# Seven block products in place of eight for most of the down-projection of a decoder layer, and the residual kept with tokens on partitions

## The chip, the core and the metric

The kernel runs on one core of one Trainium2 chip, in one launch. Its time is the device time of that core in microseconds; where several runs are given, their median. Five engines work side by side, each through its own queue in program order: TensorE (PE, with PEld for its weight loads), VectorE (DVE), ScalarE (ACT), GpSimd (POOL) and SyncE (SP, which issues all DMAs here). They wait for each other by semaphores.

## What is computed

One decoder layer on 256 tokens, with 16 meta tokens ahead of them as further keys: a norm, an input projection, eight heads of differential attention and eight of stick-breaking attention, an output projection and an MLP with a squared ReLU. D_MODEL is 2048 and D_FF 8192, all in float32.

```python
u = _rmsnorm(h, g_mix[l])
proj = jnp.einsum('bld,de->ble', u, w_in[l])
...
mixed = jnp.concatenate([o_diff, o_sb], axis=-1)
h = h + jnp.einsum('ble,ed->bld', mixed, w_out[l])

m = _rmsnorm(h, g_mlp[l])
hid = jnp.square(jax.nn.relu(jnp.einsum('bld,df->blf', m, w_up[l])))
h = h + jnp.einsum('blf,fd->bld', hid, w_down[l])
```

## The kernel before

**Float32 products in parts.** Each operand is split into a leading part `hi` (type fp32r) and the rest `lo`. A product is the sum of hi·hi, hi·lo and lo·hi. For the weights ACT makes `hi` by a cast (L164) and DVE makes `lo` by a subtraction (L166), for every tile that arrives.

**The weight stream.** All weights pass once through one stream of units, numbered in the order of use (list `order`). A unit is a tile of 128 partitions x 4 x 256 elements (512 KB): one DMA on SP into one of five buffers `raw` (RAW), then the split into one of three pairs `whi`, `wlo` (PARTS), then products. `fetch` and `later` (L203, L845) issue the load of a unit when the raw buffer five units back has been split. `part` and `halves` (L213, L220) issue the split of a unit when PE is done with the unit three back.

**The stages.** 24 strips of four units are the input projection, with attention woven in; 8 strips the output projection ("out"); then four rounds of 8 strips "up" and 8 strips "down" (ROUNDS = 4). In the last three kinds the weights are the stationary operand, and the moving operand has the tokens in its columns: `products` (L806) issues, for each 128x128 block of weights, one product of 512 columns (`whi` with both parts of the activation, side by side) and one of 256 (`wlo` with the leading part), so 768 columns. The result has output features on partitions. The residual is kept in the same form, in `xT` (features on partitions, tokens in the free dimension).

**Leaving PSUM.** PSUM has four banks "acc" for the stream and four "att" for attention. A strip uses two of "acc". `residual` (L714) adds both halves of a bank to `xT` with two DVE operations; `out_evac` (L724) then also makes `m` (the scaled operand of up, in two parts) and sums squares for the norm; `mlp_norm` (L743) makes the norm's factor `R2` as a row for each token; `up_evac` (L765) adds the halves, applies ReLU and R2, squares, and splits into `hid`; `down_evac` (L779) adds to the residual and in the last round sends 128 KB out for every 128 features.

**What sets the order.** Every engine issues in the order of the program, and that order comes from the planner `Pace` (L39). It keeps an estimated time for PE, DVE and ACT (`T`, `V`, `A`). The products of the stream are written one after another; between them `pump` writes the next steps of side jobs that are due by the estimates, trying the lanes in the order "fetch", "weights", "once", "evac", "head". So a due split of weights is written ahead of a due evacuation.

```python
    def V(self, n, rate=0.96, after=0.0):
        self.dve = max(self.dve, self.pe, after) + n / rate + 65
        return self.dve + self.WAIT
```

In `out`, the first two strips take turns (`units`), so that the last heads of attention have more products ahead of the first use of their result in `mixed`.

## Time and profile before

| what | value |
|---|---|
| median of 3 runs | 1163.44 us (1162.42 to 1163.62) |
| span of the profiled execution | 1161.0 us, first to last instruction of the core |
| time around that span | not in the profile; the median of the runs is 2.4 us above it |
| bytes read from HBM | 204.39 MB |
| input projection with attention | from the start to 340 us |
| output projection and MLP | 340 to 1157 us |

The page gives for each engine its busy time, the span in 40 slices, the chain of work that ended last, and the costliest groups of instructions by line. A row of the timeline has the start and the duration in us, the engine, the line, the operation, what is written from what is read, and the shape; in brackets stands the idle time before it and what ended that. Matmuls overlap in their records (a 256-wide one lasts 0.28 us and the next starts earlier), so the cost of one in a row is the distance between two starts. A row of the table of windows has the stretch, its length, the busy time of PE, PEld, DVE, ACT and POOL with the number of instructions, the granted clock of PE, the DMA share and the GB/s.

### The profile page before, as it was taken

The numbers are of one execution on the slowest core, as the hardware profiler recorded it, in microseconds if no ns is written. First come the engines' busy times: TensorE is split into PE (matmuls) and PEld (weight loads), VectorE is DVE, ScalarE is ACT, GpSimd is POOL, SyncE is SP. The second block draws the span as 40 slices with busy tenths as digits, with TensorE's granted clock in tenths as the row PEclk, the third lists the DMA queues.
The fourth block names the chain that finished last, engine by engine and source line by source line (L and its number), as shares of the span: only waits on it lengthen the run. The fifth ranks groups of instructions, "written<-read, shape, count | busy, mean of one in ns | idle before, by whom it ended". The sixth has DMA issues, their size and how long they took to land.

```text
span 1161.0 us, 18961 instructions
## 1 busy us (share of the span) xinstructions
PE 1153.8 (99%) x7393; PEld 1040.0 (90%) x7393; DVE 784.5 (68%) x1287; ACT 660.0 (57%) x1131; POOL 1.1 (0%) x8
## 2 busy tenths in 40 slices
PE   8999999999999999999999999999999999999998
PEld 7999999999998888888888888888888888888887
DVE  6998987887877767656555665555566555656654
ACT  7769888779675545554334554334555333555332
POOL 0000000000000000000000000000000000000000
PEclk9999999999999999999999999999999999999999
DMA  8544444444545555555555555555555555555662
GB/s 324 190 144 140 146 146 146 164 158 136 178 136 173 186 192 185 182 189 189 184 184 188 190 182 185 189 189 182 186 192 184 182 188 191 183 183 190 198 219 82
DMA packets 58986, 207.73 MB, mean 179 GB/s; under 512 B 6672, under 2 KB 8848, under 8 KB 58896
## 3 DMA queue, kind: packets, MB, share of 16 engines
q1 hardware_dynamic: 58896, 206.52, 51.5%
q8 instruction: 58, 0.95, 0.3%
q14 instruction: 32, 0.26, 0.1%
HBM read 204.39 MB, written 2.10 MB: 178 GB/s over the span
## 4 chain that ended last, share of the span: by engine, by line
PE 99%; DMA 0%; SPq 0%; DVE 0%; ACT 0%; issue 0%
PE acc L821 47%; PE acc L820 24%; PE acc L815 8%; PE acc L817 8%; PE acc L816 8%; PE s_d L539 1%; PE po_s L579 1%; PE po_d L579 1%; PE z_s L539 0%; DMA raw<-in_win 0%; PE pq_dq L467 0%; PE pv_s L516 0%; PE pv_d L516 0%; SPq L199 0%; PE pn_s L275 0%; PE pn_d L274 0%
## 5 line engine op out<-in xcount | busy, mean ns | idle before, releaser
L166 DVE TENSOR_TENSOR wlo<-raw,whi 128x1024 fp32r<-128x1024 f32 (+1 forms) x390 | 470.2, 1207 | 328.4 <-ACT whi L164 323.7
L164 ACT CAST whi<-raw 128x1024 fp32r<-128x1024 f32 (+1 forms) x390 | 403.5, 1036 | 428.9 <-PE acc L821 399.4
L821 PE MATMUL acc<-hid,whi 128*128 128x512 f32 x1024 | 357.5, 399 | 0.0
L821 PE MATMUL acc<-m,whi 128*128 128x512 f32 x1024 | 357.3, 398 | 0.0
L820 PE MATMUL acc<-hid,wlo 128*128 128x256 f32 x1024 | 277.2, 281 | 0.0
L820 PE MATMUL acc<-m,wlo 128*128 128x256 f32 x1024 | 277.2, 281 | 0.0
L815 PE MATMUL acc<-u,whi 128*128 128x272 f32 (+1 forms) x768 | 223.7, 291 | 2.0 <-ACT whi L164 2.0
L821 PEld LDWEIGHTS acc<-hid,whi 128*128 128x128 f32 x1024 | 188.3, 188 | 41.6
L821 PEld LDWEIGHTS acc<-m,whi 128*128 128x128 f32 x1024 | 188.3, 188 | 41.4
L817 PE MATMUL acc<-u,wlo 128*128 128x272 f32 (+1 forms) x768 | 220.1, 287 | 0.4 <-DVE wlo L166 0.4
L816 PE MATMUL acc<-u,whi 128*128 128x272 f32 (+1 forms) x768 | 219.7, 286 | 0.0
L820 PEld LDWEIGHTS acc<-hid,wlo 128*128 128x128 f32 x1024 | 193.3, 189 | 6.4
L820 PEld LDWEIGHTS acc<-m,wlo 128*128 128x128 f32 x1024 | 193.3, 189 | 6.4
L815 PEld LDWEIGHTS acc<-u,whi 128*128 128x128 f32 x768 | 144.8, 189 | 3.6 <-ACT whi L164 2.7
L817 PEld LDWEIGHTS acc<-u,wlo 128*128 128x128 f32 x768 | 144.7, 188 | 1.0 <-DVE wlo L166 1.0
L816 PEld LDWEIGHTS acc<-u,whi 128*128 128x128 f32 x768 | 145.2, 189 | 0.0
L821 PE MATMUL acc<-mixed,whi 128*128 128x512 f32 x256 | 89.8, 399 | 0.0
L820 PE MATMUL acc<-mixed,wlo 128*128 128x256 f32 x256 | 69.3, 281 | 0.0
L821 PEld LDWEIGHTS acc<-mixed,whi 128*128 128x128 f32 x256 | 47.1, 188 | 10.1
L820 PEld LDWEIGHTS acc<-mixed,wlo 128*128 128x128 f32 x256 | 48.3, 189 | 1.5
L767 ACT COPY ut<-acc 128x256 f32<-128x256 f32 x64 | 23.7, 370 | 15.2 <-PE acc L821 15.2
L773 DVE SCALAR_TENSOR_TENSOR ut<-ut,R 128x256 f32<-128x256 f32 x64 | 27.0, 422 | 1.1
(400 smaller groups left out, 795.2 us busy)
## 6 DMA issues: line engine op xcount, KB each, us to landing
raw<-in_wup SPq DMA_DIRECT2D x128, 512.0 KB, 3.3
raw<-in_wdn SPq DMA_DIRECT2D x128, 512.0 KB, 3.3
raw<-in_win SPq DMA_DIRECT2D x95, 512.0 KB, 3.4
raw<-in_wout SPq DMA_DIRECT2D x32, 512.0 KB, 3.3
out<-xT SPq DMA_DIRECT2D x16, 128.0 KB, 1.7
xT<-in_x SPq DMA_DIRECT2D x3, 544.0 KB, 8.8
cst<-in_cst SPq DMA_DIRECT2D x1, 673.0 KB, 10.3
xT<-in_x SPq DMA_DIRECT2D x2, 272.0 KB, 3.5
```

Source lines behind the costliest of these rows:

```text
L164: nc.scalar.copy(hi, src)
L166: nc.vector.tensor_tensor(lo, src, as32(hi), op=ALU.subtract)
L539: nc.tensor.matmul(dst, lhsT=q[x][rows, cols], rhs=k[y][rows, :n], start=i == 0, stop=i == 2)
L579: nc.tensor.matmul(o, lhsT=l, rhs=r, start=i == 0, stop=i == len(todo) - 1)
L767: nc.scalar.copy(t, o[:, SEQ:])
L773: nc.vector.scalar_tensor_tensor(t, t, 0.0, R2, op0=ALU.max, op1=ALU.mult)
L815: nc.tensor.matmul(o, lhsT=h, rhs=xh, start=first, stop=False)
L816: nc.tensor.matmul(o, lhsT=h, rhs=xl, start=False, stop=False)
L817: nc.tensor.matmul(o, lhsT=l, rhs=xh, start=False, stop=last)
L820: one = lambda: nc.tensor.matmul(out[j][:, SEQ:], lhsT=l, rhs=act[:, k, 0, :], start=False, stop=False)
L821: two = lambda: nc.tensor.matmul(out[j], lhsT=h, rhs=act[:, k, :, :], start=first, stop=last)
```

## The change

**Down in eight rounds, with seven products for eight.** ROUNDS becomes 8 (each of 1024 hidden features), and a round is split into four column groups u of 512 output features. In the first three groups of rounds 0 to 6 (`FAST`) the 2x2 blocks (two token halves, two column halves, two halves of the contraction) are multiplied by Strassen's scheme: seven block products. The activations are now the stationary operand (128 tokens), the weights the moving one, and the result has tokens on partitions. A block product is three matmuls of 256 columns (`triple`). The fourth group and the whole of round 7 stay plain: three matmuls of 512 columns for each of four pairs.

The scheme needs sums of blocks. For the weights `fast_a` splits three blocks of a unit (768 elements), then makes four sums in place in `raw` by three DVE operations; `fast_b` splits those four sums as a second unit of the stream, without a load of its own. For the activations `up_evac` makes four sums by three DVE operations and splits eight blocks instead of four. The seven results of a group are kept in an SBUF tile Z[u] over the rounds: `fast_evac` copies (round 0, ACT) or adds (DVE) four banks "att" into it. After round 6 `combine` forms the four blocks from the seven (seven DVE operations) and adds them to the residual, scaled by R2 (four more).

**Tokens on partitions.** The residual is a new tile H (two halves of 128 tokens x 2048 features), loaded once more from HBM as a separate input of 2 MB. The out products have activations as stationary operand too, three matmuls of 512 columns. `out_evac` adds to H, sums squares on ACT, transposes H by PE (32 of 128x128) and makes `m` from the transposes. R2 is now one factor for each token, applied where down is added to H, not before the square: R2 is squared already there (no root is taken).

**Up** has weights stationary as before, now as three matmuls of 256 columns (`triple2`). Up of round r+1 and down of round r take turns in the stream, in each group: up, up, down, up, down, up, down, down.

**Buffers and planner.** From the MLP on there are four parts instead of three, and a lead of three units. The estimates of `V` and `A` carry 140 and 180 ns for each operation instead of 65 and 93, and a product 0.461 ns for a column. In the output projection the strips no longer take turns.

```diff
-ROUNDS = 4
+ROUNDS = 8
+PAIRS = 4
+MLP_PARTS = 4
+MLP_LEAD = 3
+FAST = {(r, u) for r in range(ROUNDS - 1) for u in range(3)}
...
+    for r in range(ROUNDS):
+        for u in range(4):
+            for c, p in (((0, 1), (0,)), ((2,), (1,)), ((3,), (2, 3))):
+                order += up(r + 1, u, c) + down(r, u, p)
...
+    def fast_a(g, hi, lo):
+        while (g, 0) not in raw_at or ring[g] >= 0 and ring[g] not in done_at:
+            yield pc.pe + 200, None
+        yield max(raw_at[g, 0], done_at.get(ring[g], 0.0)), "a"
+        raw = raws[g]
+        t = yield from split(hi[:, 1:4], lo[:, 1:4], raw[:, 1:4], 768)
...
+        first = raw[:, 0:1].to_broadcast([P, 2, 256])
+        nc.vector.tensor_tensor(raw[:, 3::-3], first, raw[:, 3:1:-1], op=ALU.add)
+        pc.V(512)
+        nc.vector.tensor_tensor(raw[:, 2], raw[:, 3], raw[:, 2], op=ALU.add)
+        pc.V(256)
+        nc.vector.tensor_tensor(raw[:, 1], raw[:, 2], raw[:, 1], op=ALU.add)
+        pc.at["sums", g] = pc.V(256)
+
+    def fast_b(g, hi, lo):
...
+        t = yield from split(hi, lo, raws[g - 1], 1024)
...
+    def up_evac(r, i, o):
+        x = mtile("hx", [P, FULL, P], f"hx_{r}_{i}", 2)
+        nc.scalar.activation(x[:, 0:4].rearrange("p a b -> p (a b)"), o, AF.Relu)
...
+        nc.scalar.activation(x[:, 0:4], x[:, 0:4], AF.Square)
...
+            nc.vector.tensor_tensor(x[:, 4:7:2], x[:, 0:2], x[:, 1:4:2], op=ALU.subtract)
+            nc.vector.tensor_tensor(x[:, 5], x[:, 4], x[:, 3], op=ALU.add)
+            nc.vector.tensor_tensor(x[:, 7], x[:, 2], x[:, 5], op=ALU.subtract)
...
+        nc.scalar.copy(hi, x)
+        nc.vector.tensor_tensor(lo, x, as32(hi), op=ALU.subtract)
...
+    def fast_evac(r, u, o):
+        for i in range(4):
+            n = 512 if i < 3 else 256
+            dst = z[:, 512 * i : 512 * i + n]
+            if new:
+                nc.scalar.copy(dst, o[i][:, :n])
+            else:
+                nc.vector.tensor_tensor(dst, o[i][:, :n], dst, op=ALU.add)
+            pc.give("att", t)
+        if r == LAST_FAST[u]:
+            yield from combine(u)
...
+    def triple(out, x, w, first, last, check=False):
+        for i, (a, b) in enumerate(((0, 0), (1, 0), (0, 1))):
+            nc.tensor.matmul(
+                out, lhsT=x[a], rhs=w[b], start=first and i == 0, stop=last and i == 2, skip_group_check=check
+            )
...
+            if p == 0 and what == "a":
+                open_strips["down", r, u] = banks("att", 4 if fast else 2, f"down_{r}_{u}")
+            if fast:
+                todo = ((0, 0, 0, 2), (1, 0, 2, 1), (3, 0, 7, 3)) if what == "a" else (
+                    (0, 1, 6, 0), (2, 1, 4, 3), (2, 0, 5, 2), (1, 1, 3, 1))
+                for at, half, slot, q in todo:
+                    t = triple(o[at][:, 256 * half : 256 * half + 256], x(slot), (hi[:, q], lo[:, q]),
+                               p == 0 and (at, half) in ((0, 0), (1, 0), (3, 0), (2, 1)), p == PAIRS - 1, True)
```

In the rows below `whi_290_9601` is the leading part of unit 290 (the last number is the buffer's), `z_0` is Z of group 0, `down_3_1_2` the third bank of round 3, group 1, and a wait names the engine.

On DVE, before, where a strip of down ends and the next one runs (round 0, strip 41):

```order
L166 TENSOR_TENSOR wlo_169_6927<-raw_169_6824,whi_169_6926 128x1024 [waits DMAHW2_49,PE_49,Activation_49]
L718 TENSOR_TENSOR ht_508359.6666666666_2_6940<-acc_41_0_6855,xT_78 128x256 [waits PE_49]
L719 TENSOR_TENSOR xT_78<-acc_41_0_6855,ht_508359.6666666666_2_6940 128x256 [waits DVE_49]
L718 TENSOR_TENSOR ht_509659.6666666666_3_6958<-acc_41_1_6856,xT_78 128x256 [waits PE_49]
L719 TENSOR_TENSOR xT_78<-acc_41_1_6856,ht_509659.6666666666_3_6958 128x256 [waits DVE_49]
L166 TENSOR_TENSOR wlo_170_6954<-raw_170_6849,whi_170_6953 128x1024 [waits DMAHW3_49,Activation_49]
```

On DVE, now, where group 0 of round 3 has ended and group 1 begins:

```order
L893 TENSOR_TENSOR z_0_6548<-down_3_0_0_9422,z_0_6548 128x512 [waits PE_49]
L893 TENSOR_TENSOR z_0_6548<-down_3_0_1_9423,z_0_6548 128x512 [waits PE_49]
L171 TENSOR_TENSOR wlo_292_9652<-raw_292_9559,whi_292_9651 128x1024 [waits DMAHW5_49,PE_49,Activation_49]
L171 TENSOR_TENSOR wlo_291_9619<-raw_290_9481,whi_291_9618 128x1024 [waits Activation_49]
L171 TENSOR_TENSOR wlo_293_9685<-raw_293_9579,whi_293_9684 128x768 [waits DMAHW6_49,PE_49,Activation_49]
L261 TENSOR_TENSOR raw_293_9579<-raw_293_9579 128x2x256 [waits DVE_49]
L263 TENSOR_TENSOR raw_293_9579<-raw_293_9579 128x256 [waits DVE_49]
L265 TENSOR_TENSOR raw_293_9579<-raw_293_9579 128x256 [waits DVE_49]
L893 TENSOR_TENSOR z_0_6548<-down_3_0_2_9424,z_0_6548 128x512
L893 TENSOR_TENSOR z_0_6548<-down_3_0_3_9425,z_0_6548 128x256
```

The emptying of the banks is now four operations with six others between the second and the third, and each unit of a Strassen group brings up to four DVE operations where it brought one.

On PE, before, where a strip of down begins (strip 42; it takes two banks "acc"):

```order
L821 MATMUL acc_41_1_6856<-hid_0_5898,whi_167_6882 128x512
L821 MATMUL acc_42_0_6951<-hid_0_5898,whi_168_6904 128x512 [waits Activation_49]
L820 MATMUL acc_42_0_6951<-hid_0_5898,wlo_168_6905 128x256 [waits DVE_49]
L821 MATMUL acc_42_0_6951<-hid_0_5898,whi_168_6904 128x512
L820 MATMUL acc_42_0_6951<-hid_0_5898,wlo_168_6905 128x256
```

On PE, now, the begin of group 1 of round 3 (units 290 and 291, behind two units of up), from the second of its banks on:

```order
L1030 MATMUL down_3_1_1_9697<-whi_290_9601,hid_3_8556 128x256 [waits DVE_49]
L1030 MATMUL down_3_1_1_9697<-whi_290_9601,hid_3_8556 128x256
L1030 MATMUL down_3_1_1_9697<-wlo_290_9602,hid_3_8556 128x256
L1030 MATMUL down_3_1_3_9699<-whi_290_9601,hid_3_8556 128x256 [waits DVE_49]
L1030 MATMUL down_3_1_3_9699<-whi_290_9601,hid_3_8556 128x256
L1030 MATMUL down_3_1_3_9699<-wlo_290_9602,hid_3_8556 128x256
L1030 MATMUL down_3_1_0_9696<-whi_291_9618,hid_3_8556 128x256 [waits Activation_49]
L1030 MATMUL down_3_1_0_9696<-whi_291_9618,hid_3_8556 128x256
L1030 MATMUL down_3_1_0_9696<-wlo_291_9619,hid_3_8556 128x256
L1030 MATMUL down_3_1_2_9698<-whi_291_9618,hid_3_8556 128x256 [waits DVE_49]
```

The first products of a group now name waits for DVE on the bank, where before the first product of a strip waited for ACT's part alone and the second for DVE's.

On PE, before, around the last head's norm product (`pn_s31`) in the output projection; the first product that needs that head's `mixed` stands 52 rows farther on:

```order
L274 MATMUL pn_s31_5141<-oh_s31_5109,ones_99 128x256 [waits PE_49,Activation_49]
L275 MATMUL pn_s31_5141<-ol_s31_5110,ones_99 128x256 [waits DVE_49]
L821 MATMUL acc_25_1_5115<-mixed_80,whi_99_5026 128x512
L820 MATMUL acc_25_1_5115<-mixed_80,wlo_99_5027 128x256
L821 MATMUL acc_25_0_5114<-mixed_80,whi_100_5070 128x512
```

The same place on PE, now:

```order
L331 MATMUL pn_s31_5196<-oh_s31_5186,ones_99 128x256 [waits PE_49,Activation_49]
L332 MATMUL pn_s31_5196<-ol_s31_5187,ones_99 128x256 [waits DVE_49]
L1030 MATMUL out_0_0_4885<-whi_103_5062,mixed_80 128x512 [waits Activation_49]
L1030 MATMUL out_0_0_4885<-whi_103_5062,mixed_80 128x512 [waits DVE_49]
L1030 MATMUL out_0_0_4885<-wlo_103_5063,mixed_80 128x512
```

The product that needs the last head now follows its norm product directly.

More of the change, by code (lines that the diff above doesn't have):

```diff
@@ L220, in halves @@
+    def fast_b(g, hi, lo):
+        while ("sums", g - 1) not in pc.at or ring[g] >= 0 and ring[g] not in done_at:
+            yield pc.pe + 200, None
+        yield max(pc.at["sums", g - 1], done_at.get(ring[g], 0.0)), "a"
+        t = yield from split(hi, lo, raws[g - 1], 1024)
+        for kk in range(4):
+            pc.at["w", g, kk] = t
+        parted.add(g - 1)
     def halves(g, hi, lo, pieces):
@@ L790, in strip_start, with banks @@
+    def banks(tag, n, name):
+        while sum(t <= pc.pe for t in pc.banks[tag]) < n:
             pc.pe += 100
             pc.pump()
-        pc.banks["acc"] = sorted(pc.banks["acc"])[2:]
-        if what == "out" and b == 0:
-            m = big.tile([P, KT, 2, SEQ], F32R, tag="act", name="m")
-        if what == "up" and b == 0:
-            hid[a] = big.tile([P, KT, 2, SEQ], F32R, tag="mix", name=f"hid_{a}")
-        return [bank("acc", f"acc_{s}_{j}") for j in range(2)]
-    def needs(what, a, k):
-        if what == "out":
-            return [("mixed", k)]
-        if what == "up":
-            return [("m", k)]
-        return [("hid", a, k)] if what == "down" else [("u", k)]
+        pc.banks[tag] = sorted(pc.banks[tag])[n:]
+        return [bank(tag, f"{name}_{j}") for j in range(n)]
@@ L806, in products, with strip_start @@
+    def strip_start(s):
+        return banks("acc", 2, f"acc_{s}")
     def products(s, out, j, k, kk, hi, lo):
@@ L817, in products @@
             nc.tensor.matmul(o, lhsT=l, rhs=xh, start=False, stop=last)
-            return pc.T(3 * (n / 2.4 + 2.5))
-        act = {"out": lambda: mixed, "up": lambda: m, "down": lambda: hid[a]}[what]()
-        one = lambda: nc.tensor.matmul(out[j][:, SEQ:], lhsT=l, rhs=act[:, k, 0, :], start=False, stop=False)
-        two = lambda: nc.tensor.matmul(out[j], lhsT=h, rhs=act[:, k, :, :], start=first, stop=last)
-        for f in (one, two) if last else (two, one):
-            f()
-        return pc.T(768 / 2.4 + 5)
+            return pc.T(3 * 0.461 * n)
     seen_kinds = set()
@@ L897, in hymba_layer, with after, triple2 @@
             done_at[g] = pc.pe
+    def after(t, gen):
+        yield t, None
+        yield from gen
+    def triple2(out, w, x, first, last):
+        for i, (a, b) in enumerate(((0, 0), (0, 1), (1, 0))):
+            nc.tensor.matmul(out, lhsT=w[a], rhs=x[:, b], start=first and i == 0, stop=last and i == 2, skip_group_check=True)
+        return pc.T(3 * 0.461 * SEQ)
+    def triple(out, x, w, first, last, check=False):
[3 more added lines that the diff above has]
+            )
+        n = out.shape[-1]
+        return pc.T(3 * 0.461 * n)
```

380 lines of the change are left out of this document (250 added, 130 removed).

## The prediction

> **What bounds the kernel now.** I read the first part of the page, the clock row and the chain of work that ended last, then a table of two stretches (one of the input projection, one of the MLP), and last who waits for whom.
>
> ```profile
> span 1161.0 us, 18961 instructions
> PE 1153.8 (99%) x7393; PEld 1040.0 (90%) x7393; DVE 784.5 (68%) x1287; ACT 660.0 (57%) x1131; POOL 1.1 (0%) x8
> ...
> PEclk9999999999999999999999999999999999999999
> ...
> GB/s 324 190 144 140 146 146 146 164 158 136 178 136 173 186 192 185 182 189 189 184 184 188 190 182 185 189 189 182 186 192 184 182 188 191 183 183 190 198 219 82
> ...
> PE 99%; DMA 0%; SPq 0%; DVE 0%; ACT 0%; issue 0%
> ```
> ```profile
> 200.00:300.00 100.00, 100.00 (x837) 99.08 (x837) 84.48 (x179) 79.42 (x174) 0.00 (x0) 1.00 0.46 158
> 700.00:800.00 100.00, 100.00 (x569) 86.72 (x568) 57.71 (x74) 39.27 (x42) 0.00 (x0) 1.00 0.54 187
> ```
> ```profile
> ACT whi L164 <- PE acc L821: 399.4, 274, 3.3
> DVE wlo L166 <- ACT whi L164: 323.7, 285, 1.6
> ```
>
> The chain is 99% PE, and PE is busy in every slice: the time is the sum of the products at full clock. In the MLP (second table row: sum and PE, PEld, DVE, ACT) DVE is busy 58% and ACT 39%. The two waits say why: ACT's cast of the next weights waits for PE to give a part buffer back, and DVE's low part waits for that cast. Both stand ahead of PE with time to spare. So a change pays if it takes columns from PE, as long as DVE and ACT keep that lead.
>
> **What PE gains.** A product costs its distance to the next start.
>
> ```profile
> 274.73 0.28 PE L815 MATMUL acc<-u,whi 128*128 128x256 f32 x1
> ...
> 279.94 0.28 PE L817 MATMUL acc<-u,wlo 128*128 128x256 f32 x1
> ```
> ```profile
> 705.64 0.40 PE L821 MATMUL acc<-hid,whi 128*128 128x512 f32 x1
> ...
> 709.88 0.40 PE L821 MATMUL acc<-hid,whi 128*128 128x512 f32 x1
> ...
> 334.81 0.27 PE L548 MATMUL pa_s<-cst,z_s 128*128 128x128 f32 x1
> ...
> 335.13 0.27 PE L556 MATMUL pm_s<-cst,z_s 128*16 128x128 f32 x1
> ```
> ```profile
> L820 PE MATMUL acc<-hid,wlo 128*128 128x256 f32 x1024 | 277.2, 281 | 0.0
> L820 PE MATMUL acc<-m,wlo 128*128 128x256 f32 x1024 | 277.2, 281 | 0.0
> L820 PE MATMUL acc<-mixed,wlo 128*128 128x256 f32 x256 | 69.3, 281 | 0.0
> ```
>
> In the first pair 44 products of 256 columns lie between the two starts: 5.21/44 = 0.1184 us. In the second, 12 pairs of 512 and 256: 4.24/12 = 0.3533, which leaves 0.2349 for 512. A 128x128 transpose takes 0.107. The 256-wide rows come with one weight load for each product (PEld 99% in that stretch), as the new kernel's do, so that form is priced as it will run. From the counts of the new order:
> - up: 3072 of 256 = 363.7, before 1024 x 0.3533 = 361.8: +1.9
> - down: 1764 of 256 and 528 of 512 = 208.9 + 124.0 = 332.9, before 361.8: -28.9
> - out: 384 of 512 = 90.2, before 256 pairs = 90.4: -0.2
> - 32 transposes of H: +3.4; the two norm products of `mlp_norm` go: -0.2
>
> PE's work falls by **24.0 us**.
>
> **What DVE must now do.** I price a DVE operation in the same way.
>
> ```profile
> 102.01 1.22 DVE L166 TENSOR_TENSOR wlo<-raw,whi 128x1024 fp32r<-128x1024 f32 x1
> 103.14 0.42 DVE L166 TENSOR_TENSOR mixed<-oa_d,mixed 128x256 fp32r<-128x256 f32 x1
> 103.48 0.42 DVE L700 TENSOR_TENSOR o_d<-o_d,os_d 128x256 f32<-128x256 f32 x1
> ...
> 107.14 0.44 DVE L441 TENSOR_TENSOR sq_dk<-pk_dk,E 128x272 f32<-128x272 f32 x1
> 107.49 1.22 DVE L166 TENSOR_TENSOR wlo<-raw,whi 128x1024 fp32r<-128x1024 f32 x1
> ...
> 109.78 0.44 DVE L446 TENSOR_TENSOR sq_dk<-sq_dk,rw_dk 128x272 f32<-128x272 f32 x1
> 110.25 0.44 DVE L447 SCALAR_TENSOR_TENSOR sq_dk<-sq_dk,rb_dk 128x272 f32<-128x272 f32 x1
> 110.73 0.44 DVE L448 TENSOR_TENSOR ra_dk<-ra_dk,sq_dk 128x272 f32<-128x272 f32 x1
> ```
> ```profile
> L605 DVE TENSOR_TENSOR s_d<-s_d,cst 128x256 f32<-128x256 f32 x16 | 6.8, 424 | 0.2 <-PE s_d L539 0.2
> ```
>
> 1.13 us for 1024 elements and 0.34 for 256; on the line through both, 0.87 for 768, 0.60 for 512, 0.21 for 128. A PSUM operand costs nothing more (L441: 0.35 for 272), nor a broadcast one (L605: 424 ns against 420). An operation that needs the one before it starts 0.47 after it instead of 0.35 (L446 to L448): **0.12** more. I price the strided, broadcast sum of the change (L261) as a plain 512 add; it could not be below the 0.34 of 256, nor, by L605, much above 0.60.
>
> A group here is one column group u of one round: four up units and four down steps. In a Strassen group DVE has
> - 4 up units: 4 x 1.13 = 4.5
> - 4 `fast_a`: 0.87, 0.60, 0.34, 0.34 and three dependences = 2.51 each: 10.0
> - 4 `fast_b`: 4.5
> - the hidden sums and low part: 0.34 + 0.21 + 0.21 + 2 x 0.12 + 1.13: 2.1
> - the four additions to Z: 3 x 0.60 + 0.34: 2.1
>
> together **23.3 us**. PE needs 4 x 24 x 0.1184 + 4 x 21 x 0.1184 = **21.3 us**. So in three groups of four DVE is the slower engine, by 2 us; in the plain fourth PE needs 22.6 and DVE about 12.5, and it catches up, but no farther ahead than the ring of four parts lets it.
>
> The Trainium skill ("VectorE: DVE Perf Modes", section "The DRAIN you can't avoid") states that a semaphore between DVE operations costs nothing extra, since the pipe empties after each anyhow. By that the 0.12 would go, 14 times a group, and a group would need 21.6. The rows differ: 0.35 without and 0.47 with a dependence.
>
> **Where PE waits.** ACT needs 1.05 for a cast of 1024, and DVE starts 0.03 after it ends.
>
> ```profile
> 730.46 1.05 ACT L164 CAST whi<-raw 128x1024 fp32r<-128x1024 f32 x1 [1.65 <-PE acc L821]
> ```
> ```profile
> 731.54 1.23 DVE L166 TENSOR_TENSOR wlo<-raw,whi 128x1024 fp32r<-128x1024 f32 x1 [1.47 <-ACT whi L164]
> ```
>
> I take round 3 with unit numbers of the order, t = 0 where PE begins unit 276, DVE ahead after the plain group. Unit 281 may be cast when PE has ended 277 (5.7). The cast (0.8 by its length), its low part and sums (2.5), the cast of 282 (1.05) and some 0.3 of hand-overs end at 10.4. From there DVE never rests: lows 282, 283 (2.3); 284, 286 with sums (5.0); 285 (1.1), ended at 18.9. PE wants it at 17.65: **1.2 us** lost. Then the hidden sums (1.0), lows 287, 288, hidden, 289 (4.5), 290 with sums (2.5), two Z additions (1.2), 292, 291 (2.3), 293 with sums (2.5), third Z addition (0.6): it ends at 33.5. PE comes to the third product of 290 (`down_3_1_3`) at 28.9. All four "att" banks belong to a Strassen group, so this product needs a bank that `fast_evac` has not read yet: the PE rows shown with the change name a DVE wait there, and since the low part of 291 behind it names none, that wait stands for a DVE row at or behind `wlo_291`. That is the third or fourth Z addition: **4.6 us** lost. Behind the waiting product stands the whole PE queue; ACT's cast of 294 waits for unit 290 to be given back, so DVE rests 1.4 meanwhile and the delay is not won back. The second group repeats it (0.7 at 297, 4.6 at 302), the third loses 0.8 at 309. Sum for a round: **12 us**.
>
> Round 0 copies to Z on ACT, so no such bank wait: 3 us. Rounds 1 to 5: 60. Round 6 adds `combine` (seven additions and four scaled ones, by the prices above about 4.8 us for each u), two of three inside Strassen groups, half in DVE's rests: 12 + 6 = 18. Together **81 us**. Round 7 is plain: 0.
>
> **The boundary of input and output projection.**
>
> ```profile
> 353.86 0.28 PE L274 MATMUL pn_s<-oh_s,ones 128*128 128x256 f32 x1
> ```
> ```profile
> L164 ACT CAST mixed<-oa_s x8: 393/404/407, 130.5 to 358.3; 128x256 fp32r<-128x256 f32 x8
> L166 DVE TENSOR_TENSOR mixed<-oa_s,mixed x8: 414/418/419, 132.2 to 359.6; 128x256 fp32r<-128x256 f32 x8
> ```
>
> From the last head's norm product to `mixed` there are 4 to 6 us of ACT and DVE work. Before, some 50 rows of PE lie between; now the next row needs it. About 3.5 us there and 1.5 for the head before it: **5 us**, between 2 and 9.
>
> **At nothing.** The load of H is 2 MB, one DMA on SP ahead of weight loads; five raw buffers are some 14 us of PE work, and DMA is busy 46% there. At the 324 GB/s of the first slice it takes 6.5 us: without cover that would be lost. The input projection runs the same instructions in another order; DVE at 84% did not stop PE there, so 0, at worst a few us. Behind the last product stand one 512 addition and 256 KB out, against two additions of 256 and 128 KB; by the two rows below the DMA takes between 1.7 and 3.3 instead of 1.7, the addition 0.3 less: within 1.3 us, taken as 0.
>
> ```profile
> raw<-in_wup SPq DMA_DIRECT2D x128, 512.0 KB, 3.3
> ...
> out<-xT SPq DMA_DIRECT2D x16, 128.0 KB, 1.7
> ```
>
> **Rivals.**
> - *DVE keeps up* (faster). The 84% row speaks for it: a busy DVE beside a PE that never waits. It decides when a group's DVE work falls to PE's, 21.3 of 23.3, so if these operations run 9% below my prices. Then only the boundary is left: 1161.0 - 24.0 + 5 + 2.4 = **1144**. Against it: the prices come from a stretch just as dense.
> - *The bank wait does not bite*, only the work does (Z additions done earlier, or that wait meant an earlier row). DVE then runs through: from 10.4 the rest of the first group (10.5) and two groups of 23.3, to 67.6, where PE wants the low part of 311 at 62.7: 4.9 a round. 2 + 5 x 4.9 + 8 = 34: **1178**.
> - *The clock falls in the long waits.* No PE wait of this trace is near 4.6 us, and the clock is 9 in every slice, so the rows bound the loss only from below, at 0. If PE ran at half clock after each of the 12 bank waits for as long as it had waited, that is 2.3 each, 28 in all: **1253**. The Trainium skill ("TensorE: Matmul & The Clock Gate", section "Why this matters for your kernels") says that gaps over about 3 us can return the clock to half; no run here shows it yet.
>
> **How the numbers follow.** 1161.0 - 24.0 + 81 + 5 = 1223 of span; the median of the runs is 2.4 above the span of the one profiled, so **1225 us**, 5% slower. Chances: forecast 0.60; bank wait absent 0.15; clock 0.15; DVE keeps up 0.07; between that and the second rival, about where it was, 0.03. The range reaches from the second rival to the third, 1178 to 1253. A change under 0.2% can't be told from none here: faster 0.07, same 0.03, slower 0.90.
>
> **What would show it.** PE's share falls to some 92%; the list of waits has PE `down` for DVE `z` with 10 to 14 waits of 3 to 6 us, and for DVE `wlo` many of about 1; DVE is busy over 95% in the three Strassen groups of a round and about 55% in the plain one; rounds 1 to 5 take 98 us each, where products alone take 86.5. If DVE shows rests beside a PE that doesn't wait, my DVE prices were wrong; if `z` never releases PE, the bank reading was; a clock under 1.00 behind waits is the third rival.

## The result, and the profile after

| | before | after |
|---|---|---|
| median (runs) | 1163.14 us (4) | 1246.33 us (4), 1245.77 to 1247.81 |
| ratio, 95% interval | | 1.0719, 1.0704 to 1.0734 |
| span of the profiled execution | 1161.0 us | 1246.0 us |
| first product of up starts at | 433.55 us | 446.19 us |
| from there to the start of the last product | 723.4 us | 795.6 us |

The change makes the kernel 7.2% slower; the forecast was 1225 us. The last two rows are read from PE's timeline. By the prediction's own terms they should have been 441.6 (433.55 + 5 at the boundary + 3.4 of transposes - 0.4) and 777.4 (723.4 + 1.9 - 28.9 + 81). So 4.6 us are missing ahead of the MLP and 18.2 in it.

The page after, first the engines' shares, then the granted clock in 40 slices, then the chain of work that ended last:

```profile
span 1246.0 us, 21676 instructions
PE 1163.2 (93%) x8563; PEld 1109.2 (89%) x8563; DVE 981.0 (79%) x1517; ACT 726.2 (58%) x1127; POOL 1.1 (0%) x8
...
PEclk8999999999999999999899989989989998998999
...
PE 35%; DVE 21%; issue 4%; ACT 3%; DVEq 0%; ACTq 0%
```

The view of waits after (engine, its line, what it waited for: sum in us, times, longest):

```profile
PE down L1030 <- DVE z L893: 49.3, 12, 4.3
PE down L1030 <- DVE wlo L171: 18.7, 24, 1.5
```

PE is still the busiest engine, but the chain, followed back from the end to 458.6 us, is 35% PE and 21% DVE where it was 99% PE: in the MLP the end is set by the two in turns. The 12 long waits are the bank waits of the prediction (two in each of rounds 1 to 6; eleven last 4.24 to 4.26 us, the last one 2.46), the 24 short ones the low parts. The eights in the clock row, none of which the kernel before has, are new as well. One round on PE after (start, duration, what, and in brackets the idle time and its releaser):

```profile
704.52 0.39 PE L1030 MATMUL down<-wlo,hid 128*128 128x256 f32 x1 [1.29 <-DVE wlo L171]
...
714.62 0.28 PE L1030 MATMUL down<-wlo,hid 128*128 128x256 f32 x1
719.14 0.80 PE L1030 MATMUL down<-whi,hid 128*128 128x256 f32 x2 [4.24 <-DVE z L893]
719.74 0.41 PE L1030 MATMUL down<-wlo,hid 128*128 128x256 f32 x1
719.95 0.63 PE L1030 MATMUL down<-whi,hid 128*128 128x256 f32 x2
...
724.43 0.43 PE L1024 MATMUL up<-m,whi 128*128 128x256 f32 x2
...
733.50 0.39 PE L1030 MATMUL down<-wlo,hid 128*128 128x256 f32 x1 [0.54 <-DVE wlo L171]
...
748.13 0.60 PE L1030 MATMUL down<-whi,hid 128*128 128x256 f32 x2 [4.25 <-DVE z L893]
...
751.88 0.40 PE L1024 MATMUL up<-m,whi 128*128 128x256 f32 x2
...
761.66 0.39 PE L1030 MATMUL down<-wlo,hid 128*128 128x256 f32 x1 [0.54 <-DVE wlo L171]
...
806.94 0.38 PE L1030 MATMUL down<-wlo,hid 128*128 128x256 f32 x1 [1.49 <-DVE wlo L171]
```

The waits in brackets are 1.3, 4.2, 0.5, 4.3, 0.5; foretold were 1.2, 4.6, 0.7, 4.6, 0.8. Since the records of products overlap, a bracket shows less than is lost: from 714.62 to 719.14 are 4.52 us, 4.40 more than a product takes. By the starts the five are 1.6, 4.4, 0.8, 4.4, 0.8, together the 12 us foretold. But a round takes 806.94 - 704.52 = 102.4 us instead of 98.

The difference stands in the rows behind the two long waits. Behind the first, from 719.95 to 724.43, there are seven threes of products in 4.48 us, 0.64 for each three, where three take 0.36 at full speed. From 719.14 on, 24 products pass in 5.29 us; at the distance that the prediction measured they take 24 x 0.1184 = 2.84, so 2.45 us are lost. Behind the second, 18 products pass from 748.13 to 751.88, in 3.75 us instead of 2.13, so 1.6 are lost. The pair comes again in every round from 1 to 6, so that some 6 x (2.45 + 1.6) = 24 us are lost behind the waits. The table of windows names the reason, in the granted clock (the number behind POOL's count), first for another wait of 4.26, which ended at 616.89, then for the short one of round 6:

```profile
616.00:617.00 1.00, 0.11 (x1) 0.11 (x1) 1.00 (x3) 0.00 (x0) 0.00 (x0) 0.50 0.69 270
...
621.00:622.00 1.00, 1.00 (x7) 1.00 (x7) 0.60 (x1) 0.37 (x1) 0.00 (x0) 0.50 0.82 127
622.00:623.00 1.00, 1.00 (x10) 1.00 (x10) 0.63 (x1) 0.00 (x0) 0.00 (x0) 0.96 0.92 377
...
1158.00:1159.00 1.00, 0.97 (x4) 0.97 (x5) 0.97 (x3) 0.80 (x1) 0.00 (x0) 0.50 0.19 74
```
```profile
1158.03 0.80 PE L1030 MATMUL down<-whi,hid 128*128 128x256 f32 x2 [2.46 <-DVE z L893]
```

PE is idle for 4.3 us, the clock falls to 0.50 and comes back only when PE has been busy for 5.3 us, behind the second wait of a round 3.6. This is what the third rival foresaw, and 24 us are near its size (28). The Trainium skill ("TensorE: Matmul & The Clock Gate", section "Why this matters for your kernels") asks for no idle gaps above some 3 us between bursts of products. The trace agrees for the waits of 4.2 us and for those of up to 1.5, which cost nothing behind them. But the wait of 2.46 was followed by 0.50 too, so the measurement decides that 3 us is no safe bound here.

The prediction tied the length of the half clock to the length of the wait. The rows tie it to something else: the waits of 4.25 us are followed by 5.3 or by 3.6 us of it, and the returns to full clock lie whole steps of 3.41 us apart (from 724.43 it is 8 steps to 751.7, 30 to 826.8, 128 to 1161.4). Run 8 below has its MLP 13.3 us earlier, and there it is about 3 us behind the first wait of a round and 5.7 behind the second. So the length seems to depend on where a wait lies between such instants; this is read from the times, no run tested it by itself.

DVE after, at the same place, shows which addition the bank waits for:

```profile
718.06 0.42 DVE L265 TENSOR_TENSOR raw<-raw 128x256 f32<-128x256 f32 x1
718.40 1.01 DVE L893 TENSOR_TENSOR z<-down,z 128x512 f32<-128x512 f32 x2
721.10 1.23 DVE L171 TENSOR_TENSOR wlo<-raw,whi 128x1024 fp32r<-128x1024 f32 x1 [1.68 <-ACT whi L169]
```

The two at 718.40 are the third and fourth additions to Z, and PE goes on at 719.14, between their ends. Behind them DVE rests 1.68 us, since ACT's cast waits for PE: the two engines hold each other up. So in the three Strassen groups of round 3 DVE is busy for 88, 80 and 82% of the time (windows from 685.5, 708.28 and 737.25 us), not over 95%, and in the plain one, from 765.4 to 788, for 72%, not 55%. DVE's work itself is the foretold one: 82.5 us from 704.52 to 806.94, against 3 x 23.3 + 12.5 = 82.4.

Ahead of the MLP, PE after (first the start, then the boundary of input and output projection):

```profile
8.84 0.58 PE L941 MATMUL acc<-u,wlo 128*128 128x256 f32 x1 [2.57 <-DVE wlo L171]
...
364.43 0.33 PE L605 MATMUL pa_s<-cst,z_s 128*128 128x128 f32 x1 [2.12 <-ACT z_s L733]
...
370.20 0.50 PE L1030 MATMUL out<-whi,mixed 128*128 128x512 f32 x1 [0.26 <-DVE mixed L171]
...
374.59 0.96 PE L1030 MATMUL out<-whi,mixed 128*128 128x512 f32 x2 [2.72 <-ACT mixed L169]
```
```profile
8.00:10.00 2.00, 1.16 (x5) 1.16 (x6) 1.39 (x3) 0.20 (x2) 0.00 (x0) 0.50 0.99 373
...
12.00:14.00 2.00, 2.00 (x11) 2.00 (x11) 2.00 (x5) 1.65 (x5) 0.00 (x0) 0.50 1.03 421
```

The boundary waits 5.1 us, as foretold (5), and shortly after its waits of 2.12 and 2.72 the clock is at 0.50 for some 3.4 us each, which costs 3.4 more. The start, priced at nothing, has a wait of 2.57 and half the clock from 8 to 14 us: 84 products start in the first 20 us, before 110, so 26 x 0.1184 = 3.1 us are lost. DVE's rows say why, first of after, then of before:

```profile
7.27 0.92 DVE L163 SCALAR_TENSOR_TENSOR u<-xT,par,u 128x272 fp32r<-128x272 f32 x2 [1.52 <-ACT u L162]
8.10 1.29 DVE L171 TENSOR_TENSOR wlo<-raw,whi 128x512 fp32r<-128x512 f32 x2
```
```profile
5.68 0.69 DVE L166 TENSOR_TENSOR wlo<-raw,whi 128x512 fp32r<-128x512 f32 x1
6.93 0.91 DVE L158 SCALAR_TENSOR_TENSOR u<-xT,par,u 128x272 fp32r<-128x272 f32 x2 [0.56 <-ACT u L157]
```

The first low part of the weights stood ahead of the second pair of activations; now it stands behind it, 2.4 us later, and PE's product of 8.84 waits for it.

### The profile page after: what moved, and what is told of

Its sections match the earlier page's. It is cut to its first block, busy times and chain, and to the rows that moved or that the text cites. A ratio compares the mean times of both kernels' runs of the same rounds, so it can differ in the third digit from the quotient of the medians.

```text
span 1246.0 us, 21676 instructions
## 1 busy us (share of the span) xinstructions
PE 1163.2 (93%) x8563; PEld 1109.2 (89%) x8563; DVE 981.0 (79%) x1517; ACT 726.2 (58%) x1127; POOL 1.1 (0%) x8
## 4 chain that ended last, share of the span: by engine, by line
PE 35%; DVE 21%; issue 4%; ACT 3%; DVEq 0%; ACTq 0%
PE up L1024 18%; PE down L1030 17%; DVE wlo L171 11%; DVE raw L261 4%; ACT whi L169 3%; DVE raw L263 2%; DVE z L893 2%; DVE raw L265 1%; DVE hid L862 1%; DVE hx L850 0%; DVE hx L852 0%; ACT hx L842 0%; DVEq L171 0%; DVE H L870 0%; ACT hid L860 0%
## 5 line engine op out<-in xcount | busy, mean ns | idle before, releaser
L169 ACT CAST whi<-raw 128x1024 fp32r<-128x1024 f32 (+2 forms) x474 | 467.3, 999 | 450.1 <-PE up L1024 156.2
L171 DVE TENSOR_TENSOR wlo<-raw,whi 128x1024 fp32r<-128x1024 f32 (+2 forms) x474 | 542.0, 1161 | 195.4 <-ACT whi L169 194.1
L1030 PE MATMUL down<-whi,hid 128*128 128x256 f32 (+1 forms) x1528 | 337.8, 317 | 49.3 <-DVE z L893 49.3
L1024 PE MATMUL up<-m,whi 128*128 128x256 f32 x2048 | 374.6, 285 | 1.2 <-DVE m L807 0.9
L1024 PEld LDWEIGHTS up<-m,whi 128*128 128x128 f32 x2048 | 324.3, 194 | 3.4 <-DVE m L807 1.1
L1030 PEld LDWEIGHTS down<-whi,hid 128*128 128x128 f32 x1528 | 257.8, 199 | 64.7 <-DVE z L893 51.7
L1024 PE MATMUL up<-m,wlo 128*128 128x256 f32 x1024 | 290.6, 284 | 0.0
L1030 PE MATMUL down<-wlo,hid 128*128 128x256 f32 (+1 forms) x764 | 244.1, 319 | 18.7 <-DVE wlo L171 18.7
L1024 PEld LDWEIGHTS up<-m,wlo 128*128 128x128 f32 x1024 | 198.3, 194 | 0.0
L1030 PEld LDWEIGHTS down<-wlo,hid 128*128 128x128 f32 x764 | 152.6, 200 | 31.0 <-DVE wlo L171 23.6
```

The lines of the kernel that those rows point to most:

```text
L169: nc.scalar.copy(hi, src)
L171: nc.vector.tensor_tensor(lo, src, as32(hi), op=ALU.subtract)
L1024: nc.tensor.matmul(out, lhsT=w[a], rhs=x[:, b], start=first and i == 0, stop=last and i == 2, skip_group_check=True)
L1030: nc.tensor.matmul(out, lhsT=x[a], rhs=w[b], start=first and i == 0, stop=last and i == 2, skip_group_check=check)
```

## The experiments

Theory after the result: in the MLP, DVE's work (23.3 us a Strassen group against PE's 21.3) and the four banks that one group holds make the waits, and the clock makes them dearer; ahead of the MLP something in the new order costs 12.6 us. Rivals: that the clock costs nothing by itself; that the bank wait is only DVE's lateness in another dress; that the boundary's loss comes from the strips no longer taking turns. Ratios are to the kernel before, 1162.79 us in these runs (1162.75 for run 11). The two columns "up to up" and "MLP" are the two stretches of the table above.

| run | what | us | ratio, 95% interval | up to up | MLP |
|---|---|---|---|---|---|
| 1 | two of the four banks from "acc" | 1188.39 | 1.0221, 1.0204 to 1.0238 | 445.2 | 737.1 |
| 2 | PE busy in the long waits | 1225.54 | 1.0539, 1.0523 to 1.0554 | 445.7 | 775.3 |
| 3 | all groups plain | 1171.14 | 1.0067, 1.0052 to 1.0082 | 442.9 | 719.9 |
| 4 | Strassen in two groups | 1176.96 | 1.0120, 1.0105 to 1.0135 | 446.1 | 725.1 |
| 5 | before, with the new estimates | 1175.75 | 1.0111, 1.0096 to 1.0126 | 447.1 | 723.6 |
| 6 | weight sums on GpSimd | 1277.27 | 1.0996, 1.0956 to 1.1036 | 444.8 | 824.0 |
| 7 | 1 and 6 together | 1275.85 | 1.0974, 1.0956 to 1.0992 | 445.1 | 824.1 |
| 8 | old estimates up to the MLP | 1233.96 | 1.0614, 1.0597 to 1.0632 | 432.9 | 794.5 |
| 9 | 8 and 1, even order | 1181.75 | 1.0164, 1.0149 to 1.0179 | 433.4 | 742.1 |
| 10 | 9, Strassen in two groups | 1151.71 | 0.9906, 0.9891 to 0.9921 | 433.2 | 712.5 |
| 11 | 8, all groups plain | 1159.73 | 0.9972, 0.9961 to 0.9983 | 433.7 | 720.0 |

### 1. Two banks from the other tag

```diff
-open_strips["down", r, u] = banks("att", 4 if fast else 2, f"down_{r}_{u}")
+open_strips["down", r, u] = (banks("acc", 2, f"downa_{r}_{u}") if fast else []) + banks("att", 2, f"down_{r}_{u}")
...
-            pc.give("att", t)
+            pc.give("acc" if i < 2 else "att", t)
```

> The first two of the four banks of a Strassen group come from the four banks "acc" instead of "att", so no product of a group needs a bank that the group before it has just filled; all else as in the change. Theory (bank wait, and the clock that falls behind it): the 12 waits of PE for z (49 us) go, DVE's excess work stays as waits for low parts of some 5 us a round in place of 2.7, and with no wait over 3 us in the MLP the granted clock there is 1.00: 1187 us. Rival (the bank wait only shows DVE's backlog, and would come back at the low parts in full): waits for low parts of some 11 us a round, only the clock is won: 1218 us. Second rival (the clock falls for another reason than the waits): 1215 us with the clock still at 0.97.

Measured: 1188.39, in the MLP with 34 waits for `wlo` (20.6 us) and one for `z`, of 5.2 us, in round 6, behind which the clock is at 0.50 once more. PE of this run, and a window of two Strassen groups:

```profile
600.63 0.39 PE L1030 MATMUL downa<-wlo,hid 128*128 128x256 f32 x1 [0.79 <-DVE wlo L171]
612.13 0.39 PE L1030 MATMUL downa<-wlo,hid 128*128 128x256 f32 x1 [0.55 <-DVE wlo L171]
624.01 0.39 PE L1030 MATMUL downa<-wlo,hid 128*128 128x256 f32 x1 [0.60 <-DVE wlo L171]
```
```profile
692.00:738.00 46.00, 44.03 (x360) 42.80 (x360) 45.04 (x64) 26.36 (x31) 0.00 (x0) 1.00 0.57 184
```

The banks alone were worth 58 us. What is left is mostly DVE's own load, and it has the predicted size: from 600.63 to 624.01 one Strassen group takes 23.4 us, the 23.3 of the sum of DVE's operations, and DVE is busy for 45.04 of the 46 us of two such groups. A round takes 91.2 us (582.25 to 673.5), 4.7 more than the 86.5 that the prediction has for its products, about the 5 expected and not the 11 of the rival, so the backlog does not come back in full at the low parts. So the bank wait is a second cause beside DVE's lateness, and its 4.2 us are the price of four banks for each of two groups in a row. Whether it would go as well if the additions to Z stood earlier in DVE's order was not tried.

### 2. The same waits with the clock kept up

Ahead of the product that waits, PE multiplies zeros into a free bank.

```diff
+                    if at == 3 and p == 0 and u and r:
+                        fill = banks("acc", 1, f"fill_{r}_{u}")[0]
+                        for _ in range(13):
+                            nc.tensor.matmul(fill, lhsT=idle[:, :P], rhs=idle, start=True, stop=True)
+                        pc.give("acc", pc.pe)
```

> The change with 13 extra products of 512 columns (of zeros, into a bank that nobody reads) ahead of the product that waits for z, in the 12 places where it waits; the waits themselves stay. Theory (the clock falls because PE stands idle for over 3 us): PE idles under 2 us there, the clock stays at 1.00 behind the 12 places, 2.5 us less in each, of which DVE's backlog takes back some 7 us in all: 1222 us. Rival (the clock falls for another reason, or the half clock does not cost time since DVE is the bound): 1246 us or more.

PE of this run, at the same place in the same round as above:

```profile
710.59 2.98 PE L1095 MATMUL fill<-idle 128*128 128x512 bf16 x13
714.99 0.50 PE L1030 MATMUL down<-whi,hid 128*128 128x256 f32 x2 [1.42 <-DVE z L893]
715.33 0.28 PE L1030 MATMUL down<-wlo,hid 128*128 128x256 f32 x1
715.45 0.40 PE L1030 MATMUL down<-whi,hid 128*128 128x256 f32 x2
```

The useful product stands 4.40 us behind the fill's start (710.59 to 714.99), so the delay of the bank is what it was, but from 715.33 on a product takes 0.12 us at once. The kernel does more work and is 20.8 us faster: the clock is a cost of its own. In the MLP 20.3 of its 24 us are won (795.6 to 775.3). The rest is accounted for: the waits for `wlo` in down grow from 18.7 to 20.4 us in brackets, by some 3 us by the starts, and a half clock that costs some 1.3 us is left, behind a wait of 1.89 in round 6.

### 3 and 4. No Strassen group, and two

```diff
-FAST = {(r, u) for r in range(ROUNDS - 1) for u in range(3)}
+FAST = set()
```

> No Strassen groups: all column groups plain, all the rest of the change as it is (residual with tokens on partitions, eight rounds, four parts, planner). Theory: no wait of PE in the MLP, PE's products as before plus 5 us, boundary 5 us with 3 us of low clock behind it, start 4 us: 1182 us. Rival (the new layout with its transposes and its 1024-wide evacuation is what costs): over 1200 us.

```diff
-FAST = {(r, u) for r in range(ROUNDS - 1) for u in range(3)}
+FAST = {(r, u) for r in range(ROUNDS - 1) for u in (0, 2)}
```

> Strassen in column groups 0 and 2 of each round alone, with a plain group behind each: no two Strassen groups follow each other. Theory: no wait for z, one wait for a low part of about 1.4 us in each Strassen group, products 14 us less than before, boundary and start as in the change: 1183 us. Rival (each Strassen group costs its share of the change's loss wherever it stands, two thirds of 83 us): 1215 us.

Both came out below what was expected, 1171.14 and 1176.96. Without Strassen nothing waits in the MLP but for 1.2 us at its start, and the MLP takes 719.9, 3.5 less than before, where the prediction's prices make it 0.9 more (up + 1.9, and 1536 products of 512 in down, 360.8 against 361.8). Experiment 11 shows why, at the end of the output projection, where 512-wide products follow each other, and at the start of up:

```profile
427.81 0.39 PE L1031 MATMUL out<-whi,mixed 128*128 128x512 f32 x1
...
433.48 0.39 PE L1031 MATMUL out<-wlo,mixed 128*128 128x512 f32 x1
```
```profile
434.06 0.40 PE L1025 MATMUL up<-m,whi 128*128 128x256 f32 x2
...
436.94 0.40 PE L1025 MATMUL up<-m,whi 128*128 128x256 f32 x2
```

25 starts in 5.67 us are 0.227 for 512 columns (priced 0.2349), and 24 in 2.88 are 0.120 for 256 (priced 0.1184). Over the whole MLP of run 3 the means are 0.23 and 0.119: the 512-wide product was priced too high, the 256-wide one rightly. With two groups no bank wait is left; a plain group takes two banks, and it gives the additions time. The 18.5 us of waits in down are for `wlo` alone, in 14 places. And the stretches up to up, 442.9 and 446.1 us, are 9.4 and 12.5 too long, so that most of this loss is not Strassen's. In run 3's profiled execution the same two waits at the boundary (2.12 and 2.72 us) left the clock at 1.00, which would account for most of the difference between the two.

### 5. The estimates alone

The kernel before, with the change's estimates and nothing else:

```diff
-        self.dve = max(self.dve, self.pe, after) + n / rate + 65
+        self.dve = max(self.dve, self.pe, after) + n / rate + 140
...
-        self.act = max(self.act, self.pe, after) + n / 1.2 + 93
+        self.act = max(self.act, self.pe, after) + n / 1.2 + 180
...
-            return pc.T(3 * (n / 2.4 + 2.5))
+            return pc.T(3 * 0.461 * n)
```

> The kernel of before with nothing changed but the planner's estimates of the change (140 and 180 ns in place of 65 and 93 added to each step of VectorE and ScalarE, 0.461 ns a column for a product). These estimates also order the first strips. Theory: the waits of 0.96 and 2.57 us and the half clock from 8 to 14 us at the start of the changed kernel come from the new order, and so come with the estimates alone: the first 20 us lose about 4, and the time is 1167 us (1165 to 1170). Rival: the start's waits come from something else (where the tiles lie, the loads); then the time is that of before, 1163. Second rival: the new estimates also move the attention's steps and cost waits all through the input projection: above 1175.

Neither the size nor the place was right: 1175.75, 13 us more than before, of which the start has only some 3 (88 instead of 110 products start in its first 20 us: 22 x 0.1184 = 2.6). PE of this run at the boundary, where the kernel before has no wait at all:

```profile
363.66 0.33 PE L548 MATMUL pa_s<-cst,z_s 128*128 128x128 f32 x1 [2.39 <-ACT z_s L676]
365.00 0.50 PE L821 MATMUL acc<-mixed,whi 128*128 128x512 f32 x1 [0.58 <-DVE mixed L166]
371.15 0.39 PE L274 MATMUL pn_s<-oh_s,ones 128*128 128x256 f32 x1 [0.72 <-ACT oh_s L164]
374.72 0.58 PE L820 MATMUL acc<-mixed,wlo 128*128 128x256 f32 x1 [2.72 <-ACT mixed L164]
```

These are nearly the boundary waits of the changed kernel, to the 2.72, though the strips take turns here. Dearer estimates put the steps of the last heads later in the order, so that they reach the output projection unfinished: the last head's transposes `pa_s` start at 363.7 us here and at 364.4 in the changed kernel, before at 334.8, while the output projection begins at about 340 in all three.

### 8. The old estimates ahead of the MLP

The changed kernel, with the planner's old numbers until the first unit of up:

```diff
+        self.old = True
...
-        self.dve = max(self.dve, self.pe, after) + n / rate + 140
+        self.dve = max(self.dve, self.pe, after) + n / rate + (65 if self.old else 140)
...
+    pc.old = False
     for g in range(first_mlp, len(order)):
```

> The changed kernel with the planner's estimates of before up to the first up-projection strip, and those of the change from there on; nothing else differs, so the MLP keeps its waits of 4.25 us. The run with the new estimates alone on the kernel of before lost 13 us: some 3 at the start, 6.4 of waits and some 3 of half clock between the input and the output projection. Theory: of the changed kernel's own loss at the start (4 us) and at that boundary (5.1 of waits and 3 of half clock) the start goes wholly and most of the boundary goes, too: 1246 - 4 - 6 = 1236 us (1233 to 1240). Rival: the boundary's waits come from the output strips no longer taking turns, as predicted, and stay: 1242. Second rival: the order of the start does not matter, 1246.

1233.96, and 432.9 us up to up: the whole loss ahead of the MLP is gone, start and boundary both, and the last `pa_s` starts at 334.5 us, though the strips still don't take turns. The rival, which was the prediction's reading, falls. The MLP keeps its 794.5.

### 6 and 7. The weight sums on GpSimd

```diff
-        nc.vector.tensor_tensor(raw[:, 3::-3], first, raw[:, 3:1:-1], op=ALU.add)
+        nc.gpsimd.tensor_tensor(raw[:, 3::-3], first, raw[:, 3:1:-1], op=ALU.add)
```

and the other two sums likewise; run 7 has the banks of run 1 as well.

> The changed kernel with the three additions that make a group's weight sums on GpSimd in place of VectorE, and the four att banks as they are. VectorE then has some 2 us less by each group of products (0.99 of low halves stays, 0.73, 0.45 and 0.35 of sums go: 1.5 x 4 chunks of a strip), so it is no longer the longer engine, and the 18.7 us of waits for the low halves (wlo) go. Theory: the wait for the banks is mostly VectorE's backlog; without it the two additions that free the first banks take about 1.3 us behind the last product, 12 times 1.3 = 16 in place of 49, short enough that the clock stays full: 1137 + 16 + 8 at the boundary + 5 at the start + 1 = 1167 us. Rival: the wait is set by the order of VectorE's steps, not by its load, and stays at 4.25 with the half clock behind it: 1246 - 19 = 1227. Second rival: GpSimd's additions come late or slow VectorE's own, and TensorE waits for wlo all through the MLP: 1250 or more.

> The weight sums on GpSimd, as in the run beside this one, and two of the four banks of a Strassen group from the acc tag, as in the first experiment. Theory: both causes of waits in the MLP are gone, and what is left is TensorE's own 1137 us, 8 at the boundary, 5 at the start and 1 between output projection and up-projection: 1151 us (1147 to 1156), which is below before. Rival: VectorE's load was not what made the 22 us of short waits for wlo in the first experiment but the latency of the chain from the load to the low half; then these waits stay, 1170 to 1188. Second rival: GpSimd slows VectorE's additions where they run side by side: 1188 or more.

Both are the slowest of all. GpSimd in run 6 by groups, ACT and DVE by time:

```profile
L265 POOL TENSOR_TENSOR raw<-raw 128x512 f32<-128x512 f32 x84 | 133.9, 1594 | 868.6 <-DVE wlo L175 863.0 <-DMA raw<-in_wdn 5.6
L269 POOL TENSOR_TENSOR raw<-raw 128x256 f32<-128x256 f32 x84 | 99.2, 1181 | 6.6
L267 POOL TENSOR_TENSOR raw<-raw 128x256 f32<-128x256 f32 x84 | 80.6, 959 | 6.6
```
```profile
773.76 1.05 ACT L173 CAST whi<-raw 128x1024 fp32r<-128x1024 f32 x1 [4.35 <-POOL raw L269]
```
```profile
764.61 1.65 DVE L175 TENSOR_TENSOR wlo<-raw,whi 128x1024 fp32r<-128x1024 f32 x1 [1.63 <-ACT whi L173]
```

GpSimd is 25% busy; its load is not the trouble. One unit's three sums take 1594 + 959 + 1181 ns = 3.73 us there (1.5 on DVE), and they are a chain: low part, three sums, cast of the sums, low part of the sums. ACT's cast of the sums stands in a queue in order, and waits up to 6 us in front of casts that could run; DVE then waits for ACT (311.5 us, after the change 194.1) and PE in down for both (53.2 us for `wlo`, 31.0 for the cast). DVE's own operations get longer beside GpSimd, too, up to 1.65 us for the 1024 elements that take 1.23 otherwise, but in the mean only from 1.222 to 1.268. So the second rival holds, with the lateness as what looks like its main part; how much the two engines slow each other in all was not isolated. Run 6 has no wait of PE for `z`, with the four banks as they were, which fits a bank wait that needs a late DVE as well.

### 9, 10 and 11. The order, and the number of Strassen groups

All three have the old estimates ahead of the MLP. Runs 9 and 10 have the banks of run 1 and one chunk of up between two of down; run 10 has Strassen in groups 0 and 2, run 11 in none (with the change's order of chunks).

```diff
-            for c, p in (((0, 1), (0,)), ((2,), (1,)), ((3,), (2, 3))):
+            for c, p in (((0,), (0,)), ((1,), (1,)), ((2,), (2,)), ((3,), (3,))):
```

> The kernel beside this one (old estimates before the MLP), two banks of a Strassen group from the acc tag, and the up-projection's chunks spread evenly: one chunk of up between any two chunks of down, in place of two, one, one and none. In the experiment with the banks alone 22 us of waits for wlo stayed, in 35 places of some 0.5 to 0.8, and VectorE was 0.98 busy through the Strassen strips and under 0.5 in the plain one. Theory: VectorE is then the longer engine only for the stretch of three Strassen strips in a row (some 23.3 against 21.3 us each), which the even order does not change, but the bursts are gone: half of the 22 goes, and with the start and the boundary the time is 1188 - 11 - 10 = 1167 us (1160 to 1172). Rival: waits stay as they were, 1178. Second rival: the even order brings the additions to z in front of the low halves that are due, waits grow: 1188 or more.

> As the kernel beside this one, with two of four column groups (0 and 2) by Strassen's products in place of three, so that a Strassen strip stands between plain ones and VectorE (0.81 busy over a round in the experiment with two groups) catches up in each plain strip. TensorE then has 1161 - 16 = 1145 us of its own. Theory: the 20 us of waits for wlo in 16 places of that experiment came from the end of a Strassen strip, where two chunks of down followed each other with no up between, and go with the even order; the start and the boundary go as well: 1177 - 20 - 8 = 1149 us (1146 to 1156), below before. Rival: the waits come from the additions to z that stand ahead of the low halves in VectorE's order, whatever the chunks' order, and stay: 1167.

> The changed kernel without Strassen's products (all four column groups plain, as in the third experiment) and with the planner's estimates of before up to the MLP: what is left of the change is the tokens-on-partitions layout, the interleaved order of up and down, and the halved rounds. In the third experiment the first product of the up-projection started at 442.90 us and the last product at 1162.76, 719.9 later, against 433.55 and 723.4 in the kernel before. With the estimates of before up to the MLP that first product started at 432.9 (the run with Strassen in three groups). Theory: the parts add up, 432.9 + 719.9 + 4.2 behind the last product's start + 1.8 outside the span: 1159 us, 0.35% below before, so that of the 11 us that the version with two Strassen groups gains some 4 are the layout's and 7 Strassen's. Rival: the third experiment's MLP was short because its weights were already ahead after the slow boundary; with no stall there the MLP takes 723 or more and the time is that of before, 1162 to 1165.

Run 9 is a miss: 1181.75 instead of 1167, since its MLP (742.1) is no better than run 1's (737.1), and PE still waits 20.8 us for `wlo`. It also has one wait of 7.2 us for `z` and two of together 2.2 for ACT's copies to Z, where run 1 has the one of 5.2:

```profile
PE downa L1031 <- DVE z L894: 7.2, 1, 7.2
```

With three Strassen groups in a row DVE owes 3 x 2 us in each round, and this order inside the groups does not take that away. Run 10 has the same order with a plain group behind each Strassen group, and the waits all but go. Its view of waits, and two windows of half a round each:

```profile
PE downa L1031 <- DVE wlo L172: 3.7, 11, 0.5
```
```profile
668.00:712.00 44.00, 43.79 (x323) 41.49 (x322) 36.08 (x47) 23.76 (x26) 0.00 (x0) 1.00 0.60 192
712.00:757.00 45.00, 44.58 (x330) 42.08 (x328) 37.07 (x48) 24.58 (x28) 0.00 (x0) 1.00 0.58 188
```

A Strassen group and a plain one take DVE 36 of 44 us, and PE is all but full. **1151.71 us is 0.94% below before** (0.79 to 1.09%). Run 11 says what of that is Strassen's: the layout, the rounds and the change's order without it give 1159.73, 0.28% below before (0.17 to 0.39%), and run 10 is another 8.0 us faster. Of run 10, banks, order and estimates were not undone one by one, so the 8.0 is what Strassen's products bring together with the banks and the even order, which keep their waits down.

## Why the prediction was right or wrong

- **Direction and mechanism of the MLP: right.** That DVE becomes the longer engine in a Strassen group (23.3 against 21.3) was measured at 23.4 in run 1, and its work in a round of the changed kernel is 82.5 us against 82.4; that a third or fourth addition to Z holds a bank stands in the rows; so do the two long waits in each of rounds 1 to 6. The rivals "DVE keeps up" and "the bank wait does not bite" fall. One sign failed: DVE is not over 95% busy in the Strassen groups but 80 to 88%, since it rests behind the bank waits, and its backlog runs into the plain group.
- **The waits' sum: near.** 81 us were foretold; PE's waits for DVE in down are 49.3 + 18.7 = 68.0 by the brackets and 51 + 25 = 76 by the starts. In rounds 1 to 5 the starts give 12.3 a round, foretold 12. What was too high is round 6: 12 instead of 18, since its second bank wait is only 2.46.
- **The clock: the term that failed.** The forecast took it at 0 and gave it 0.15 as a rival; both its rival and the waits were true at once. It is 24 us by the rows behind the waits, and run 2 wins 20.3 of them. With about 693 us of products, 76 of waits, 24 of clock and 1.6 of waits at its start, the MLP comes to 795, against 795.6 measured. Since the forecast already had 12 waits of 4.6, longer than any in the trace of before, "the rows bound the loss only from below" was a reason to take a value between the two ends, not the lower one.
- **The boundary: right number, wrong reason.** 5 foretold, 5.1 of waits measured, but not because the strips no longer take turns: run 5 has the waits with turns, run 8 is without them without turns. That the number fits is luck. The falling clock adds 3.4 there as well.
- **The input projection "at 0, at worst a few us": wrong.** The changed estimates reorder it, and with the boundary they cost the whole 12.6 us ahead of the MLP. The text named the new estimates among the parts of the change but gave their order no price of its own; the order of DVE's first rows, as shown above, was there to be read.
- **PE's work: near enough.** The products of the MLP, priced at 696.4 us, take about 693, since a 512-wide one takes 0.23 instead of 0.2349.
- **The load of H and the tail at nothing: right.** No engine's wait names the load of H, and the last product starts 4.2 us ahead of the span's end, before the change 4.0.
- **The total.** 1225 against 1246.3 is as near as it is in part because terms cancel: the clock (24 us) and the loss ahead of the MLP (4.6) were missing, the waits (5) and the products (3) were too high.

## What to carry to other kernels

Before work is moved from TensorE to another engine, put that engine's sum for one group beside TensorE's and look at what lies next to it in the order: here the same scheme lost 7% with three groups in a row and four banks for each, and gained 0.9% with a plain group behind each, the banks split over two tags, an even order and the old estimates ahead of the MLP. A wait of over 4 us is priced with the half clock behind it, here 1.6 to 2.45 us more. And numbers in a planner are part of the program: estimates that were changed for one stage cost 13 us in another, which the same numbers ordered.

## What the runs showed of the hardware

- What an idle PE costs in clock is not set by its length alone. In all the runs a single idle time of up to 1.55 us was never followed by 0.50, and one of 4.2 or more always. In between it was either: 2.46 us in the changed kernel was followed by it and 2.47 in run 8 was not, both in round 6; 2.12 and 2.72 at the boundary were in the changed kernel and were not in run 3. Shorter ones close together were followed by it, too (0.82 and 0.76 us, ending at 931.27 and 932.53 in run 6).
- Behind idle times of 4.25 us the 0.50 lasted 3.6 or 5.3 us of busy time, and the returns to full clock lie whole steps of 3.41 us apart.
- A GpSimd addition of 256 elements takes 0.96 to 1.18 us in the mean beside DVE, and the low part on DVE up to 1.65 instead of 1.23 (in the mean 1.268 instead of 1.222). The Trainium skill ("SBUF — State Buffer", section "Who interferes with whom") says that a VectorE operation with two inputs in SBUF contends with a GpSimd operation that reads SBUF; both are of that kind, and the rows agree.
